# Hybrid mLSTM/attention encoder layer: which buffers hold the output projection's residual rows and its last norm scale, and what a held block waits for

## The chip, the cores and the metric

One core of one Trainium2 chip. The metric is the device time in microseconds (us) of one execution; runs of one kernel lie within about 0.3% of each other. Profile times are counted from the start of the profiled span.

## The reference

One encoder layer on two requests (2048 and 256 tokens, 2304 rows together, width 1024), all in float32:

```python
def encoder_layer(x, ...):
    h = rmsnorm(x, norm1_w)
    p = h @ w_in                                   # mq, mk, mv, mo, gates, aq, ak, av
    m_out = mlstm_mixer(mq, mk, mv, mo, gates, b_gates, mh_norm_w)   # 8 heads, both directions
    a_out = attention_mixer(aq, ak, av, q_norm_w, k_norm_w)          # 8 heads on 2 kv heads, all keys
    x = x + jnp.concatenate([m_out, a_out], axis=-1) @ w_out
    h = rmsnorm(x, norm2_w)
    u = centred_dwconv(h @ w_up, conv_w, conv_b)                     # width 3, 2 x 2816 channels
    a, g = jnp.split(u, 2, axis=-1)
    return x + (jax.nn.silu(g) * a) @ w_down       # a last rmsnorm follows
```

## The kernel before

The work is done in stages, each with its own pools of buffers, and every float32 matrix product is three products of rounded parts (high x high, low x high, high x low), so each operand is split by a ScalarE copy (the high part) and a VectorE subtraction (the low part).

- Stage a: norm statistics, queries, keys, values and gates.
- Stages b and m together: attention (`attention`, a generator over 36 blocks of one or two heads) and the mLSTM heads (`mlstm`). Both write their results to DRAM in `mix_d`.
- Stage c (`phase_c`): x + mix @ w_out. It goes over nine blocks of 256 tokens in the order `ORDER = (0, 1, 2, 3, 4, 5, 8, 6, 7)`; block 8 is the short request. It begins while attention still runs, and its matmuls fill TensorE between attention's.
- Stage d: the up-projection (`up_phase`, three token blocks of 768, each in 11 rounds `gi` of two pairs `UpPair`), with convolution and gate, and the down-projection.

**A block of stage c.** `loads` and `loads2` fetch eight tiles of mixed input (`mix`, L973 to L975: load, ScalarE copy, VectorE subtraction; blocks at even places of the order in the ring `nT`, at odd places in the ring `mx`, eight buffers each) and four tiles of x, each 128 x 512 (L985, ring `x`, `CX` = 6 buffers). `mm` makes four output slices z of 48 matmuls each (L997); two PSUM banks `po` take turns. `post` adds x to a slice on VectorE (L1004, the eviction of the bank), stores the sum to `x1_d` (L1005) and sums squares (L1007, L1011; ring `sq`, one buffer). `tail`, traced after the first slice of the block that follows, turns the sum into a scale (`rstd_bc`), multiplies the four x tiles by the norm weight and the scale (L1026) and stores them to `n2_d` (L1028). So an x buffer is free only when that store has landed.

**The last block's tail** (block 7) is `g.c_end`, called after the first matmuls of stage d (`first`, two `UpPair`s). Here `rstd_bc` runs with `act`: TensorE sums the squares (L128), ScalarE takes the root (L133), VectorE adds epsilon (L134), inverts the root and makes a Newton step (L138 to L141, tiles `rcol`, `rcol0`, `rcol1`). GpSimd stores the 256 scales to `rl_d` (L145), reads them back spread over all partitions into `rb` (L147, tag `sq`), and after ScalarE's weight (L1023) multiplies x by it (L1024) and stores it (L1028).

**Shared space.** A pool that opens takes the space of closed ones, and each new tile waits for the old tiles that lie under it. Stage c's pools lie on the right side of the buffer memory, from low to high: x, `mx`, `acc`, `sq`, the little `rcol` columns, `nT`, `raw` (weight loads), half of the weights. Stage d's first buffer of `u` (the evicted up-projection, L1168, six buffers) begins inside `acc` and ends just behind the `rcol` columns; the other five lie over `nT`. Its tiles of the gate (`y`, `ts`) lie over x and `mx`. Most operands of the first up-projections (L1087 to L1089) and the weight sums `tw` (L1122) lie over stage c's weights, so they wait for stage c's last matmul.

**The held block.** The first mixed input of the seventh block in order (block 8) is first written by a one-element cast on GpSimd (L972) from `g.hold`. `g.hold` is the tile `m4` (row maxima of the scores) of the attention block that called `prep2` last (L571), here the last of the 36; so block 8 isn't loaded before that tile is made.

**What orders the work.** Instructions are traced in program order with priorities and then put in each engine's queue by a planner that simulates the program's timeline (`schedule_with_timeline_sim`). A queue is in order: who waits holds up what is behind. Nearly all DMAs are issued by SyncE (SP).

Of the kernel before, what the change touches and what calls it, by code (L numbers as in the profile page):

```python
# [9 lines left out]
F32 = mybir.dt.float32  # L10
F32R = mybir.dt.float32r
AF = mybir.ActivationFunctionType
ALU = mybir.AluOpType
# [4 lines left out]
P = 128  # L18
# [9 lines left out]
EPS = 1e-6  # L28
# [8 lines left out]
BT = 256  # L37
NB = T // BT
NTB = 8
CX = 6  # L40
# [8 lines left out]
MXB = 8  # L49
# [13 lines left out]
ORDER = (0, 1, 2, 3, 4, 5, 8, 6, 7)  # L63
# [22 lines left out]
def f32(ap):  # L86
    return ap.bitcast(F32)
# [32 lines left out]
def rstd_bc(g, sp, pp, sqs, n, ptag, name, bufs=1, act=False):  # L120


    nc = g.nc
    k = n // P
    ps = pp.tile([P, 512], F32, tag=ptag, name="rs_" + name, bufs=bufs)
    for t in range(k):
        for i, sq in enumerate(sqs):
            nc.tensor.matmul(ps[:, 504 + 2 * t:506 + 2 * t], sq[:, t * P:(t + 1) * P], g.ones, start=i == 0,  # L128
                             stop=i == len(sqs) - 1)
    r = sp.tile([P, 4], F32, tag="rcol", name="rcol_" + name)[:, 0:k]  # L130
    if act:
        sr = sp.tile([P, 4], F32, tag="rcol0", name="rcol0_" + name, bufs=1)[:, 0:k]
        nc.scalar.activation(sr, ps[:, 504:504 + 2 * k].rearrange("p (t o) -> p t o", o=2)[:, :, 0], AF.Sqrt, bias=g.eps)  # L133
    nc.vector.tensor_scalar(r, ps[:, 504:504 + 2 * k].rearrange("p (t o) -> p t o", o=2)[:, :, 0], EPS, None, ALU.add)  # L134
    if act:
        v, r = r, sr
        u = sp.tile([P, 4], F32, tag="rcol1", name="rcol1_" + name, bufs=1)[:, 0:k]
        nc.vector.reciprocal(r, r)  # L138
        nc.vector.scalar_tensor_tensor(u, r, -0.5, r, ALU.mult, ALU.mult)
        nc.vector.tensor_tensor(u, u, v, ALU.mult)  # L140
        nc.vector.scalar_tensor_tensor(r, u, 1.5, r, ALU.add, ALU.mult)  # L141
    else:
        nc.gpsimd.tensor_tensor(r, r, g.mhalf[:, 0:k], ALU.pow)
    if act:
        nc.gpsimd.dma_start(g.rl_d.rearrange("t p -> p t"), r)  # L145
        rb = sp.tile([P, k, P], F32, tag="sq", name="rb_" + name, bufs=1)
        nc.gpsimd.dma_start(rb, g.rl_d[:].unsqueeze(0).to_broadcast([P, k, P]))  # L147
        return rb.rearrange("p t q -> p (t q)")
    for t in range(k):
        nc.tensor.matmul(ps[:, t * P:(t + 1) * P], r[:, t:t + 1].to_broadcast([P, P]), g.ident, start=True, stop=True)  # L150
    return ps[:, 0:n]
# [311 lines left out]
def attention(g, tc, s1, s2, pp):  # L463


    nc = g.nc
    sp = s1
    hbs = []
# [7 lines left out]
    def load_kv(grp, k0, k1, after=None):  # L476

        if (grp, k0) in kv:
            return
        n = k1 - k0  # L480
        sp = s2 if n == NT1 else s1
        kv[(grp, k0)] = parts = []
        for t0 in range(0, n, 4):
            m = min(4, n - t0)
            s = f"{n}_{t0}"
            kk = sp.tile([P, m * P], F32R, tag="kk" + s, name=f"kk{grp}_{s}", bufs=1)
            kl1 = sp.tile([65, m * P], F32R, tag="kl1" + s, name=f"kl1{grp}_{s}", bufs=1)
            vv = sp.tile([P, m, P], F32R, tag="vv" + s, name=f"vv{grp}_{s}", bufs=1)
            vl = sp.tile([P, m, HD], F32R, tag="vl" + s, name=f"vl{grp}_{s}", bufs=1)
            c = slice((k0 + t0) * P, (k0 + t0 + m) * P)  # L490
            if after is not None:
                for t in (kk[0:1, 0:1], kk[HD:HD + 1, 0:1], kl1[0:1, 0:1], vv[0:1, 0, 0:1], vl[0:1, 0, 0:1]):
                    nc.gpsimd.tensor_copy(t, after[0:1, 0:1])
            nc.gpsimd.memset(f32(vv[:, :, HD:P]), 1.0)
            for r in (0, HD):
                nc.gpsimd.dma_start(f32(kk[r:r + HD, :]), g.k_d[grp, 0:HD, c])
            nc.gpsimd.dma_start(f32(kl1[0:HD, :]), g.k_d[grp, HD:P, c])
            nc.gpsimd.memset(f32(kl1[64:65, :]), 1.0)
            for a, t in ((0, vv[:, :, 0:HD]), (1, vl)):
                nc.gpsimd.dma_start(f32(t), g.v_d[grp, :, k0 + t0:k0 + t0 + m, a])  # L500
            parts.append((kk, kl1, vv, vl))
# [14 lines left out]
    def load_q(n):  # L516

        if n in qzs or n >= len(hbs):
            return
        t = 0  # L520
        qz = qzs[n] = sp.tile([P, 4, P], F32R, tag="qz", name=f"bq{n}", bufs=QZB)
        for h, q0, q1 in hbs[n][1]:
            nc.sync.dma_start(f32(qz[:, t:t + q1 - q0]), g.q_d[h, q0:q1].rearrange("n p d -> p n d"))
            t += q1 - q0

    def prep(n):

        s = HB()
        grp, s.qs, k0, k1 = hbs[n]
        s.last = n == len(hbs) - 1  # L530
        load_q(n)
        load_kv(grp, k0, k1)
        s.kv = kv[(grp, k0)]
        s.nq, s.nk = 4, k1 - k0
        s.N = s.nq * P
        s.nm = "%d_%d" % s.qs[0][0:2]
        qz = qzs.pop(n)
        pq = pp.tile([P, 1024], F32R, tag="sc", name="pq" + s.nm)
        for t in range(s.nq):
            nc.tensor.transpose(pq[:, t * P:(t + 1) * P], qz[:, t, :], g.identr)  # L540
        load_q(n + 1)
        s.qq = sp.tile([P, 512], F32R, tag="qq", name="qq" + s.nm, bufs=2)
        nc.scalar.activation(s.qq[:, 0:s.N], f32(pq[:, 0:s.N]), AF.Copy)
        s.qm = sp.tile([65, 512], F32R, tag="qm", name="qm" + s.nm, bufs=2)
        nc.scalar.activation(s.qm[0:HD, 0:s.N], f32(pq[0:HD, 0:s.N]), AF.Copy)
        s.mx = sp.tile([P, 4, 2], F32, tag="mx", name="mx" + s.nm, bufs=2)
        s.nsp = -(-s.nk * P // 1024)
        s.todo = [(t, z) for z in range(s.nsp) for t in range(s.nq)] if s.nk * P > 512 else [(None, 0)]
        s.steps = len(s.todo)
        return s  # L550
# [17 lines left out]
    def prep2(s):  # L568

        nq = s.nq  # L570
        s.m4 = g.hold = sp.tile([P, 4], F32, tag="m4", name="m4" + s.nm, bufs=2)  # L571
        nc.vector.tensor_reduce(s.m4[:, 0:nq], s.mx[:, 0:nq, 0:s.nsp], AX.X, ALU.max)
        m4r = sp.tile([P, 4], F32R, tag="m4r", name="m4r" + s.nm, bufs=2)
        nc.vector.tensor_scalar(m4r[:, 0:nq], s.m4[:, 0:nq], -1.0, None, ALU.mult)
        pr = pp.tile([P, 1024], F32, tag="sc", name="pr" + s.nm)
        for t in range(nq):
            nc.tensor.matmul(pr[:, t * P:(t + 1) * P], m4r[:, t:t + 1].to_broadcast([P, P]), g.identr, start=True,
                             stop=True)
        nc.scalar.activation(s.qm[HD:HD + 1, 0:s.N], pr[HD:HD + 1, 0:s.N], AF.Copy)
# [28 lines left out]
    def fin1(s):  # L608

        s.o1 = sp.tile([P, 256], F32, tag="o1", name="o1" + s.nm, bufs=1)  # L610
        s.rs = sp.tile([P, 256], F32, tag="rs", name="rs" + s.nm, bufs=1)
        for z in range(2):
            for r, o in ((0, s.o1), (HD, s.rs)):
                nc.scalar.activation(o[HD * z:HD * z + HD], s.pv[r:r + HD, 256 * z:256 * z + 256], AF.Copy)  # L614

    def fin2(s):
# [6 lines left out]
        for h, q0, q1 in s.qs:  # L623
# [6 lines left out]
            if h == 5:  # L630
                g.mixed5.update(range(q0, q1))

    cur = prep(0)
    while cur.todo:
        maxstep(cur)
        yield 0.5
    prep2(cur)
    load_kv(0, 0, NT1, cur.m4)
    pend, fins = [], []
# [311 lines left out]
def phase_c(g, sn, sp, pp, wps):  # L951
# [3 lines left out]
    nc = g.nc  # L955
# [10 lines left out]
    def mix(b, c):  # L966
        if ORDER.index(b) % 2:
            m = sp.tile([P, 2, BT], F32R, tag="mx", name=f"cmx{b}_{c}", bufs=MXB)
        else:
            m = sn.tile([P, 2, BT], F32R, tag="nT", name=f"cmx{b}_{c}", bufs=NTB)  # L970
        if (b, c) == (ORDER[6], 0):
            nc.gpsimd.tensor_copy(m[0:1, 1, 0:1], g.hold[0:1, 0:1])  # L972
        nc.sync.dma_start(f32(m[:, 1]), g.mix_d[b, :, c])  # L973
        nc.scalar.activation(m[:, 0], f32(m[:, 1]), AF.Copy)
        nc.vector.tensor_tensor(m[:, 1], f32(m[:, 1]), f32(m[:, 0]), ALU.subtract)  # L975
        return m

    def loads(b):
        return [mix(b, c) for c in range(NCC - 1)]

    def loads2(b, mx):
        mx.append(mix(b, NCC - 1))
        x = [sp.tile([P, 2, BT], F32, tag="x", name=f"cx{b}_{z}", bufs=CX) for z in range(4)]
        for z in range(4):
            nc.sync.dma_start(x[z], g.xT[b, :, 2 * z:2 * z + 2])  # L985
        return x
# [50 lines left out]
    for i, b in enumerate(ORDER):  # L1037
        yield 2 * b
        mx = pre.pop(b) if b in pre else loads(b)
        x = loads2(b, mx)  # L1040
# [623 lines left out]
```

## Time and profile before

| | |
|---|---|
| median of 3 runs | 3342.4 us (3339.56 to 3344.06) |
| profiled execution | 3341.97 us, its span 3340.3 us |
| TensorE matmul busy | 3246.0 us (97%) |
| TensorE weight loads | 3021.6 us (90%) |
| VectorE, ScalarE, GpSimd | 2426.8 us (73%), 1996.0 us (60%), 532.2 us (16%) |
| mean granted TensorE clock | 0.988 |

The profile page gives busy time by engine, 40 slices of the span with busy shares in tenths, the chain of work that ended last, and groups of instructions by source line. Its trace can be asked for an engine's instructions in order of time, for who waited for whom, and for busy time in any stretch. In such rows `<-` behind a duration in brackets names what ended the idle time ahead of an instruction.

### The profile page before, as it was taken

The numbers are of one execution on the slowest core, as the hardware profiler recorded it, in microseconds if no ns is written. First come the engines' busy times: TensorE is split into PE (matmuls) and PEld (weight loads), VectorE is DVE, ScalarE is ACT, GpSimd is POOL, SyncE is SP. The second block draws the span as 40 slices with busy tenths as digits, with TensorE's granted clock in tenths as the row PEclk, the third lists the DMA queues.
The fourth block names the chain that finished last, engine by engine and source line by source line (L and its number), as shares of the span: only waits on it lengthen the run. The fifth ranks groups of instructions, "written<-read, shape, count | busy, mean of one in ns | idle before, by whom it ended". The sixth has DMA issues, their size and how long they took to land. (4 is left out here: it accounts for less than half of the span.)

```text
span 3340.3 us, 53168 instructions
## 1 busy us (share of the span) xinstructions
PE 3246.0 (97%) x19484; PEld 3021.6 (90%) x19484; DVE 2426.8 (73%) x3751; ACT 1996.0 (60%) x3746; POOL 532.2 (16%) x927
## 2 busy tenths in 40 slices
PE   8989999999999999999998799999999999999998
PEld 7888888888888888788878799999999999999998
DVE  7855676676657778866666699998888888666664
ACT  5646666666665666754563455666666677554543
POOL 4551042223224323100000100000000000020201
PEclk9999999999999999999999899999999999999999
DMA  9973333343355444422228466668676657967673
GB/s 351 316 213 100 110 100 116 101 119 117 91 159 171 126 147 136 134 86 96 96 65 282 162 237 217 220 235 278 211 255 237 209 194 253 316 226 269 217 243 122
DMA packets 359197, 612.44 MB, mean 183 GB/s; under 512 B 31077, under 2 KB 215319, under 8 KB 358935
## 3 DMA queue, kind: packets, MB, share of 16 engines
q1 hardware_dynamic: 329431, 563.14, 50.2%
q0 software_dynamic: 11936, 34.09, 3.8%
q10 hardware_dynamic: 17568, 11.80, 1.1%
q8 instruction: 154, 2.52, 0.3%
q14 instruction: 108, 0.88, 0.1%
HBM read 444.98 MB, written 163.93 MB: 182 GB/s over the span
## 5 line engine op out<-in xcount | busy, mean ns | idle before, releaser
L593 DVE TENSOR_TENSOR xx<-pe,xx 128x1024 fp32r<-128x1024 f32 x260 | 319.3, 1228 | 165.0 <-ACT xx L592 163.6
L591 ACT ACTIVATE pe<-ps 128x1024 f32<-128x1024 f32 x260 | 266.2, 1024 | 229.4 <-PE ps L588 215.3
L566 DVE TENSOR_REDUCE mx<-px 128x1 f32<-128x1024 f32 x256 | 310.7, 1219 | 100.9 <-PE px L564 99.8
L592 ACT ACTIVATE xx<-pe 128x1024 fp32r<-128x1024 f32 x260 | 275.0, 1058 | 5.1
L1381 POOL TENSOR_TENSOR sq<-sq,sq 128x384 f32<-128x384 f32 x38 | 49.2, 1295 | 1380.2 <-ACT sq L1377 1299.2
L997 PEld LDWEIGHTS po<-cmx,wo 128*128 128x128 f32 x1728 | 232.4, 192 | 26.3 <-issue 5.5
L997 PE MATMUL po<-cmx,wo 128*128 128x256 f32 x1728 | 240.9, 285 | 8.3 <-DVE cx L1004 7.4
L1168 ACT ACTIVATE u<-pa 128x386 f32<-128x386 f32 (+2 forms) x264 | 129.2, 490 | 197.1 <-PE pa L1164 172.5
L604 PE MATMUL pv<-xx,vv 128*128 128x512 f32 x520 | 212.5, 409 | 9.7 <-ACT rs L614 6.8
L587 PE MATMUL ps<-qq,kk 128*128 128x512 f32 x520 | 213.5, 411 | 7.8 <-ACT pe L591 3.7
L606 PE MATMUL pv<-xx,vv 128*128 128x512 f32 x520 | 210.8, 405 | 4.8 <-DVE xx L593 4.8
L588 PE MATMUL ps<-qm,kl 65*128 65x512 f32 x520 | 208.6, 401 | 0.0
L605 PE MATMUL pv<-xx,vl 128*64 128x512 f32 x520 | 207.4, 399 | 0.0
L722 PEld LDWEIGHTS mj<-mn,wm 128*128 128x128 f32 x1296 | 179.8, 194 | 18.4 <-ACT og L738 4.5
L722 PE MATMUL mj<-mn,wm 128*128 128x256 f32 x1296 | 191.1, 289 | 2.8 <-ACT og L738 2.8
L732 PE MATMUL mv<-wm,mn 128*128 128x256 f32 x1296 | 189.8, 286 | 1.4 <-ACT qb L728 1.4
L732 PEld LDWEIGHTS mv<-wm,mn 128*128 128x128 f32 x1296 | 176.1, 190 | 15.3 <-ACT qb L728 2.4
L243 PE MATMUL pj<-w_a,n1T 128*128 128x512 f32 (+1 forms) x864 | 166.5, 351 | 9.5 <-ACT w_a L105 7.6
L564 PE MATMUL px<-kk,qq 128*128 128x512 f32 x512 | 167.3, 408 | 2.5 <-ACT pe L591 2.4
L1164 PE MATMUL pa<-nt,wb 128*128 128x386 f32 (+2 forms) x792 | 148.3, 342 | 19.2 <-ACT u L1168 19.2
L243 PEld LDWEIGHTS pj<-w_a,n1T 128*128 128x128 f32 x864 | 140.3, 191 | 28.8 <-ACT w_a L105 7.6
L1164 PEld LDWEIGHTS pa<-nt,wb 128*128 128x128 f32 x792 | 142.1, 192 | 19.7 <-ACT u L1168 19.7
(341 smaller groups left out, 8069.6 us busy)
## 6 DMA issues: line engine op xcount, KB each, us to landing
mn<-n_d SPq DMA_DIRECT2D x216, 256.0 KB, 3.1
ru<-w_up SPq DMA_DIRECT2D x88, 512.0 KB, 4.9
rs<-wsu_d SPq DMA_DIRECT2D x88, 512.0 KB, 5.6
act_d<-ts SPq DMA_DIRECT2D x33, 768.0 KB, 6.2
nt<-act_d SPq DMA_DIRECT2D x60, 384.0 KB, 4.9
re_t<-wsd_d SPq DMA_DIRECT2D x45, 512.0 KB, 5.3
wsu_d<-tw SPq DMA_DIRECT2D x44, 512.0 KB, 3.5
act_d<-ya SPq DMA_DIRECT2D x99, 192.0 KB, 2.1
```

Of the source, the lines that this page charges most:

```text
L243: nc.tensor.matmul(pjs[t][:, c0:c1], nTs[tiles[t]][:, c, a, :], ws[c][:, b, c0:c1], start=(c == 0 and k == 0), stop=(c == NCC - 1 and k == 2))
L566: nc.vector.tensor_reduce(s.mx[:, t0, z0:z0 + 1], ps, AX.X, ALU.max)
L587: nc.tensor.matmul(o, kk[:, kc:kc + P], s.qq, start=True, stop=False)
L591: nc.scalar.activation(pe, ps, AF.Exp)
L592: nc.scalar.activation(x[:, 0], pe, AF.Copy)
L593: nc.vector.tensor_tensor(x[:, 1], pe, f32(x[:, 0]), ALU.subtract)
L604: nc.tensor.matmul(s.pv, vv[:, kt % 4, :], x1, start=kt == 0, stop=False)
L606: nc.tensor.matmul(s.pv, vv[:, kt % 4, :], x2, start=False, stop=kt == s.nk - 1)
L722: nc.tensor.matmul(pj[:, o].rearrange("p (n t) -> p n t", t=P), s.w[c][:, a, o * P:(o + 1) * P], nT[c][:, :, h, :], start=(c + o + k == 0) ...
L732: nc.tensor.matmul(pv[:, o], nT[c][:, o, a, :], s.w[c][:, h, 256:512], start=(c + o + k == 0), stop=(c == NCC - 1 and k == 2 and o == 1))
L997: nc.tensor.matmul(po[:, o], wo[c][z // 2][:, a, n], mx[c][:, h, :], start=c + o + k == 0, stop=c == NCC - 1 and o == 1 and k == 2)
L1164: s.nc.tensor.matmul(p, w[:, aa, c, :], ops[k][:, c, bb, 0:s.n], start=c == 0 and i == 0 and not add, stop=c == NCC // 2 - 1 and i == 2, s ...
```

## The change

- The last block's four x tiles are taken from the ring `mx` (the mixed inputs'), those of the block two places before (block 8) half from `x` and half from `raw`; all others stay in `x`.
- The spread scale `rb` of the last block is taken from `mx` instead of `sq`.
- In the same tail, ScalarE reads the sum out of PSUM: it adds epsilon (Identity into `r`) and takes the root of `r`; VectorE's addition is left to the other blocks.
- `g.hold` is no longer each block's `m4`; it is the output tile `o1` (one buffer) of the third-last attention block.

```diff
     if act:
         sr = sp.tile([P, 4], F32, tag="rcol0", name="rcol0_" + name, bufs=1)[:, 0:k]
-        nc.scalar.activation(sr, ps[:, 504:504 + 2 * k].rearrange("p (t o) -> p t o", o=2)[:, :, 0], AF.Sqrt, bias=g.eps)
-    nc.vector.tensor_scalar(r, ps[:, 504:504 + 2 * k].rearrange("p (t o) -> p t o", o=2)[:, :, 0], EPS, None, ALU.add)
+        nc.scalar.activation(r, ps[:, 504:504 + 2 * k].rearrange("p (t o) -> p t o", o=2)[:, :, 0], AF.Identity, bias=g.eps)
+        nc.scalar.activation(sr, r, AF.Sqrt)
+    else:
+        nc.vector.tensor_scalar(r, ps[:, 504:504 + 2 * k].rearrange("p (t o) -> p t o", o=2)[:, :, 0], EPS, None, ALU.add)
...
         nc.gpsimd.dma_start(g.rl_d.rearrange("t p -> p t"), r)
-        rb = sp.tile([P, k, P], F32, tag="sq", name="rb_" + name, bufs=1)
+        rb = f32(sp.tile([P, 2, BT], F32R, tag="mx", name="rb_" + name, bufs=MXB))[:, 0, 0:n].rearrange("p (t q) -> p t q", t=k)
...
         grp, s.qs, k0, k1 = hbs[n]
+        s.n = n
...
-        s.m4 = g.hold = sp.tile([P, 4], F32, tag="m4", name="m4" + s.nm, bufs=2)
+        s.m4 = sp.tile([P, 4], F32, tag="m4", name="m4" + s.nm, bufs=2)
...
         s.o1 = sp.tile([P, 256], F32, tag="o1", name="o1" + s.nm, bufs=1)
+        if s.n == len(hbs) - 3:
+            g.hold = s.o1
...
         mx.append(mix(b, NCC - 1))
-        x = [sp.tile([P, 2, BT], F32, tag="x", name=f"cx{b}_{z}", bufs=CX) for z in range(4)]
+        i = ORDER.index(b)
+        if i == NB - 1:
+            x = [f32(sp.tile([P, 2, BT], F32R, tag="mx", name=f"cx{b}_{z}", bufs=MXB)) for z in range(4)]
+        else:
+            x = [sp.tile([P, 2, BT], F32, tag="x", name=f"cx{b}_{z}", bufs=CX) for z in range(2 if i == NB - 3 else 4)]
+            x += [g.raw.tile([P, 512], F32, tag="raw", name=f"cx{b}_{z}", bufs=2).rearrange("p (o t) -> p o t", o=2)
+                  for z in range(len(x), 4)]
```

## The prediction

> **What bounds the kernel now.** I read the page first (busy shares, the slices), then the chain that ended last, then stretches, TensorE's order of time around the one dip, and there the queues of the other engines.
>
> ```profile
> span 3340.3 us, 53168 instructions
> PE 3246.0 (97%) x19484; PEld 3021.6 (90%) x19484; DVE 2426.8 (73%) x3751; ACT 1996.0 (60%) x3746; POOL 532.2 (16%) x927
> PE   8989999999999999999998799999999999999998
> PEclk9999999999999999999999899999999999999999
> ```
>
> TensorE is busy 97% of the span, and the order of its work is fixed, so time comes off only where it idles or runs at a lower clock. The dip in slices 22 and 23 (about 1750 to 1920 us) is the passage from the output projection (stage c) to the up-projection (stage d). All that the diff touches stands there.
>
> ```profile
> core 0: us, PE busy (x), PEclk, DMA share, GB/s
> 1690.00:1718.50 28.50, 22.90 (x92) 1.00 0.38 117
> 1752.20:1821.30 69.10, 61.70 (x494) 0.95 0.78 267
> 1790.60:1796.00 5.40, 0.08 (x2) 0.95 0.98 337
> 1796.00:1798.00 2.00, 2.00 (x9) 0.50 0.87 308
> 1841.80:1861.00 19.20, 0.03 (x1) 0.50 0.06 7
> 1861.00:1864.00 3.00, 3.00 (x9) 0.50 0.66 225
> 1880.00:2820.00 940.00, 940.00 (x5352) 1.00 0.66 229
> ```
>
> Columns: stretch, its length, TensorE's busy time and matmuls, granted clock, DMA share, rate. Three holes: 5.6 us at the end of attention, one of 5.3, one of 19.2; behind the last two the clock is 0.50. The up-projection has no slack at all. TensorE's own rows name the releasers (in brackets: idle before, and what ended it):
>
> ```profile
> 1777.06 5.67 PE L997 MATMUL po<-cmx,wo 128*128 128x256 f32 x33 [2.08 <-DVE cx L1004]
> 1795.98 7.25 PE L997 MATMUL po<-cmx,wo 128*128 128x256 f32 x48 [5.32 <-DVE cx L1004]
> 1807.44 13.79 PE L997 MATMUL po<-cmx,wo 128*128 128x256 f32 x114
> 1837.56 4.23 PE L1164 MATMUL pc<-nt,wb 128*128 128x386 f32 x12 [3.95 <-DVE rcol_c L134]
> 1860.97 7.32 PE L1164 MATMUL pa<-nt,wb 128*128 128x386 f32 x24 [19.18 <-ACT u L1168]
> ```
>
> Undisturbed, a matmul of stage c takes 13.79/114 = 0.121 us. Stage c's matmuls end at 1807.44 + 13.79 = 1821.2; I call that point E.
>
> **The change part by part.**
>
> **1. x of the last three blocks (8, 6, 7 in stage c's order).** Before, x has six buffers and each block takes four, so block 6 gets two of its x only when block 8's normed x has been stored.
>
> ```profile
> SPq L985 <- DMA n_d<-cx: 2.7, 4, 1.9
> 1790.73 0.48 DMA cx<-xT
> 1795.14 0.70 DVE cx L1004
> 1790.25 0.96 DVE L1089 TENSOR_TENSOR nt<-nt 128x772 fp32r<-128x772 f32 x1
> ```
>
> SP waits four times for that store; the load goes out at 1790.73, and the eviction that needs it (L1004) runs at 1795.14. That is the 5.32 us. After it, blocks 8 and 6 hold 2 + 4 = 6 x buffers and block 8 two raw ones, which stage c's weights left long ago: block 6's four loads wait for block 5 alone. The last block's x goes where block 6's mixed input was, free in its last output slice (z=3). Its first eviction is wanted two slices (96 x 0.121 = 11.6 us) after its first matmul, so there is time for a load like the one above (4.4 us). Removed: 5.32, and the slow restart, 7.25 - 48 x 0.121 = 1.4. Lower end: the eviction stands in VectorE's queue behind the row of 1790.25, which ends at 1791.21; with 0.7 for itself TensorE would still idle 1.3. Ends: -6.7 and 0 (another late input); I take **-6.0**, nearest the row that frees it all. Number of DMAs and their bytes are unchanged, and two loads leave the crowded stretch (DMA share 0.98).
>
> Such a rest of 1.3 us would, by the Trainium skill (TensorE: Matmul & The Clock Gate, "Part 1: The HAM clock gate"), cost no clock, since the gate closes after an idle window of about 3.4 us. The trace disagrees: behind 2.08 us of idleness 33 matmuls took 5.67 us, 1.7 more than 33 x 0.121. By the page this part would be -5.4 at worst, by the row -3.7.
>
> **2. The 2.08 us before it** come from VectorE's queue, not from a buffer of the change:
>
> ```profile
> 1775.06 0.75 DVE L975 TENSOR_TENSOR cmx<-cmx 128x256 fp32r<-128x256 f32 x2
> 1776.32 0.68 DVE L1004 TENSOR_TENSOR cx<-po,cx 128x512 f32<-128x512 f32 x1
> ```
>
> Block 6's first eviction stands behind the last block's mixed input, which waits for block 8's matmuls. Those come earlier (part 3), so up to 2.08 + 1.7 = 3.8 can go; it can as well grow by as much as the planner puts ahead of the eviction. Ends -3.8 and +2; **-1.5**.
>
> **3. The kept block.** Block 8's first mixed input waits for a one-element cast on GpSimd that reads the tile `hold`: before, the last attention block's maxima (L572), afterwards the third-last one's output (written last by L620).
>
> ```profile
> 1699.08 0.42 DVE L620 TENSOR_TENSOR o<-o,rs 128x256 f32<-128x256 f32 x1
> 1713.87 0.15 DVE L572 TENSOR_REDUCE m<-mx 128x4 f32<-128x8 f32 x1
> 1714.15 0.18 POOL L972 CAST cmx<-m 1x1 fp32r<-1x1 f32 x1 [13.05 <-DMA cmx<-mix_d]
> 1707.03 0.49 PE L604 MATMUL pv<-xx,vv 128*128 128x512 f32 x1 [0.36 <-ACT xx L592]
> 1708.50 0.50 PE L587 MATMUL ps<-qq,kk 128*128 128x512 f32 x1 [0.76 <-DVE mx L566]
> 1711.92 0.51 PE L604 MATMUL pv<-xx,vv 128*128 128x512 f32 x1 [0.36 <-ACT xx L592]
> 1714.01 0.50 PE L606 MATMUL pv<-xx,vv 128*128 128x512 f32 x1 [1.35 <-DVE xx L593]
> 1730.04 0.38 ACT L614 ACTIVATE o<-pv 64x256 f32<-64x256 f32 x1
> ```
>
> The cast can go at 1699.5 instead of 1714.0, some 14.5 us earlier, and block 8's matmuls fill TensorE from about 1704 on. The four idle gaps after that sum to 0.36 + 0.76 + 0.36 + 1.35 = 2.8; those before stay. TensorE works without a hole from there to the end of attention, so filler used earlier is not missed later. The output tile has one buffer, so the next block's copy (L614, 1730.04) now waits for the cast: 30 us of room. Ends -2.8 and 0; **-2.5**.
>
> **4. The spread scale and the first u.** The scale rb shared the buffer of the squares, and the first u of stage d lies over that buffer (pool order and sizes in the code).
>
> ```profile
> 1835.23 0.26 ACT L133 ACTIVATE rcol_c<-rs_c,eps 128x2 f32<-128x2 f32 x1
> 1838.74 0.17 DVE rcol_c L141
> 1841.87 8.15 DMA rl_d<-rcol_c
> 1850.66 0.58 POOL L147 DMA_DIRECT2D rb_c<-rl_d  x1 [8.02 <-DMA rl_d<-rcol_c]
> 1854.90 5.49 POOL L1024 TENSOR_TENSOR cx<-cx,rb_c 128x256 f32<-128x256 f32 x8 [3.67 <-DMA rb_c<-rl_d]
> 1860.42 0.88 ACT L1168 ACTIVATE u<-pa 128x386 f32<-128x386 f32 x2 [23.40 <-POOL cx L1024]
> ```
>
> ScalarE's copy into u starts 0.03 us after GpSimd's eighth multiply with rb (1854.90 + 5.49 = 1860.39). With rb in a mixed-input buffer that wait goes. What is late next: the same u also covers the little columns behind the squares, rcol0 among them, which the store to rl_d reads. So u waits for that store to land: 1841.87 + 8.15 = 1850.0, then, as now, 0.4 for ScalarE and 0.55 to TensorE's restart: 1851.0 instead of 1860.97, **-10.0**. Ends: -23.1 (this hole and the 3.95 before it both gone) and 0 (something as late in its place). The restart at half clock stays, since about 9 us of idleness are left. The later y and ts tiles over the mixed-input buffers are written after a whole round; I cost them at nothing.
>
> The store writes single elements; the fit in the Trainium skill (DMA: Bandwidth & Descriptors), 2.0 us plus bytes over 436e3 per us, gives an estimate of 2 us, and with it u would be ready near 1844, part 4 at -16. This store's own row, 8.15, decides.
>
> **5. The sum read by ScalarE.** One Identity like the 0.26 us Sqrt is added ahead of it, one 0.15 us VectorE operation (L134) goes, and the bank that holds up TensorE at 1837.56 is free after that Identity, near 1835.5. But TensorE then only reaches the wait for u sooner. The chain to rl_d is set by VectorE's queue (L141 at 1838.74); upper end -1.9, the way from Sqrt's end (1835.49) to 1837.4, lower +0.3: **0**.
>
> **6. Crowding.** From 1752.2 to 1821.3 DMA is 0.78 x 69.1 = 54 us busy; parts 1 to 3 leave some 59 us for it. Operands for the first up-projections, all loaded at E, start behind more traffic: 0 to +3, **+1**.
>
> Sum: -6.0 - 1.5 - 2.5 - 10.0 + 0 + 1 = -19.0. The profiled execution took 3341.97 us, its span and 1.7 around it; 3341.97 - 19.0 = 3323.0. The median before, 3342.4, is 0.4 above it, so I say **3323**.
>
> **The rivals.**
>
> A. *u waits for nothing on GpSimd's side*, because the planner hands that place to a later u. For: only the first u of the phase lies there. Against: buffers were taken in this order before. The hole shrinks to what VectorE's operand splits leave: some 13 us more gain, **3310**.
>
> B. *The x stall is replaced*: SP issues in order, and the last block's x waits there for block 6's matmuls with other loads behind it, or evictions stand behind splits in VectorE's queue as in part 2. Parts 1 and 2 are lost: **3331**.
>
> C. *The change doesn't free u*: it stays blocked as long by another tile over it. Against: the 0.03 us between GpSimd's last multiply and u. Parts 1 to 3 remain: **3333**; with B too, 3340, no change.
>
> D. *Slower*: the planner orders the whole program anew, and the first of the three token blocks of the up-projection has little room on VectorE:
>
> ```profile
> 1880.00:2200.00 320.00, 320.00 (x1810) 319.85 (x1809) 299.51 (x382) 196.25 (x308) 0.00 (x0) 1.00 0.63 220
> ```
>
> Columns: TensorE, its weight loads, VectorE, ScalarE, GpSimd. VectorE is 299.5 of 320 us busy while TensorE never waits. If evictions come to stand behind splits there, each of the eleven rounds gains a hole. It takes (19.0 + 6.7)/11 = 2.3 us a round to be slower; at 3 us a round, **3356**. Against: nothing there is edited, and the order before had no hole in 940 us.
>
> **How the numbers follow.** Forecast 0.54 (its own range 3316 to 3331), A 0.13, B 0.14, C 0.08, B with C 0.04, D 0.07. The bound of what can be told from no change is 0.2%, 6.7 us. Faster: forecast, A, B and most of C, 0.86; same: the rest of C, and B with C, 0.07; slower: D, 0.07. The range 3309 to 3337 leaves out D, B with C, and the lower end of A: 0.16.
>
> **What would show it.** Right: no idle time before the last block's matmuls and loads of block 6's x well before 1790; the cast near 1700; the first u copy released by the store to rl_d, some 29 us after stage c's last matmul instead of 39; multiplies with rb running beside u. Wrong: ScalarE's first u still released by GpSimd; another releaser of 4 to 5 us before the last block; holes between 1880 and 2820.

## The result, and the profile after

The changed kernel takes 3325.2 us (median of 5 runs, 3321.4 to 3327.5) against 3342.4 of the kernel before (5 runs): a ratio of 0.9943, 95% interval 0.9926 to 0.9960. The forecast was 3323, within 3309 to 3337. One execution of a later kernel (the scale alone) took 7148.9 us, more than twice any other; it stands in no ratio.

From the page of the changed kernel: the span, the busy shares, and TensorE's busy share and granted clock in 40 slices.

```profile
span 3323.5 us, 53157 instructions
PE 3240.1 (97%) x19484; PEld 3015.5 (91%) x19484; DVE 2427.3 (73%) x3750; ACT 1993.5 (60%) x3747; POOL 533.2 (16%) x927
PE   8989999999999999999999899999999999999998
PEclk9999999999999999999999899999999999999999
```

The two slices of the dip (8 and 7 tenths) are now one slice of 8. TensorE's rows in order of time through that passage, and one stretch of the up-projection (TensorE, its weight loads, VectorE, ScalarE, GpSimd):

```profile
1777.43 4.78 PE L1008 MATMUL po<-cmx,wo 128*128 128x256 f32 x38 [1.29 <-DVE cx L1015]
1782.41 13.33 PE L1008 MATMUL po<-cmx,wo 128*128 128x256 f32 x110
1799.72 13.56 PE L1008 MATMUL po<-cmx,wo 128*128 128x256 f32 x112
1823.31 4.45 PE L1175 MATMUL pc<-nt,wb 128*128 128x386 f32 x24
1843.34 6.59 PE L1175 MATMUL pa<-nt,wb 128*128 128x386 f32 x24 [15.59 <-ACT u L1179]
```
```profile
1880.00:2820.00 940.00, 940.00 (x5354) 939.86 (x5353) 827.55 (x1013) 613.16 (x1071) 0.00 (x0) 1.00 0.67 231
```

The 5.32 us hole ahead of the last block is gone: 110 matmuls run through its start, and between 1735 and 1787 SP issues no load of x. The 3.95 us ahead of the pc group is gone as well. From E (now 1799.72 + 13.56 = 1813.28) to the restart it is 30.06 us instead of 39.74. The up-projection still has no hole, which disposes of rival D. The other engines at the two places where the change acts:

```profile
1704.49 0.80 POOL L145 TENSOR_TENSOR rcol_c<-rcol_c,mhalf 128x2 f32<-128x2 f32 x1 [43.67 <-DVE rcol_c L136]
1705.27 1.08 POOL L631 DMA_DIRECT2D mix_d<-o  x2
1706.36 0.70 POOL L977 CAST cmx<-o 1x1 fp32r<-1x1 f32 x1
...
1834.84 0.77 POOL L147 DMA_DIRECT2D rl_d<-rcol_c  x1 [37.72 <-issue]
1848.07 8.39 POOL L1035 TENSOR_TENSOR cx<-cx,rb_c 128x256 f32<-128x256 f32 x8 [4.26 <-issue]
```
```profile
1842.80 0.88 ACT L1179 ACTIVATE u<-pa 128x386 f32<-128x386 f32 x2 [12.42 <-DMA rl_d<-rcol_c]
```

The first u starts 5.3 us before the multiplies with rb begin, and is released by the store to rl_d, as forecast.

One thing does not fit. The engines' orders of instructions first differ near 1428 us (two loads of x on SP), and yet the changed kernel is 5.5 us late already at 1409. As a milestone near attention's end I take one of ScalarE's copies out of attention's last matmuls (the 67th; M below): 1691.04 before, 1696.36 after, so 5.3 us lost ahead of the kept block's cast and all that follows. The profile therefore has to be read in segments: M to E, E to TensorE's restart R (the start of the first group pa<-nt,wb), R to the end of the span. All profiles of this study (us):

| kernel | M | M to E | E to R | R to end | span |
|---|---|---|---|---|---|
| before | 1691.0 | 130.2 | 39.7 | 1479.3 | 3340.3 |
| before, again | 1697.2 | 131.0 | 40.3 | 1478.8 | 3347.4 |
| changed | 1696.4 | 116.9 | 30.1 | 1480.2 | 3323.5 |
| changed, again | 1700.1 | 119.1 | 30.7 | 1480.4 | 3330.3 |
| x alone | 1694.2 | 121.1 | 40.4 | 1477.7 | 3333.3 |
| scale alone | 1699.1 | 131.4 | 29.7 | 1484.7 | 3344.9 |
| sum alone | 1691.0 | 131.5 | 40.0 | 1478.4 | 3340.8 |
| kept block alone | 1692.3 | 125.8 | 40.4 | 1475.1 | 3333.6 |
| one column moved | 1694.4 | 117.1 | 19.3 | 1489.8 | 3320.6 |
| three columns moved | 1689.3 | 116.1 | 17.5 | 1489.3 | 3312.2 |
| clear of the first y | 1690.7 | 116.2 | 17.4 | 1478.3 | 3302.5 |
| tie to the fifth-last | 1701.6 | 116.8 | 32.3 | 1476.6 | 3327.2 |
| tie to the fourth-last | 1696.7 | 123.0 | 28.5 | 1477.8 | 3326.0 |

In the last two rows M itself is moved by the edit: 532 and 561 of stage c's matmuls come behind it, 576 in the kernels before and changed, so their M and M to E can't be compared with the other rows.

### The profile page after: what moved, and what is told of

Its sections match the earlier page's. It is cut to its first block, busy times and chain, and to the rows that moved or that the text cites. A ratio compares the mean times of both kernels' runs of the same rounds, so it can differ in the third digit from the quotient of the medians.

```text
span 3323.5 us, 53157 instructions
## 1 busy us (share of the span) xinstructions
PE 3240.1 (97%) x19484; PEld 3015.5 (91%) x19484; DVE 2427.3 (73%) x3750; ACT 1993.5 (60%) x3747; POOL 533.2 (16%) x927
## 5 line engine op out<-in xcount | busy, mean ns | idle before, releaser
L607 PE MATMUL pv<-xx,vv 128*128 128x512 f32 x520 | 212.5, 409 | 11.3 <-ACT rs L619 7.1
L245 PEld LDWEIGHTS pj<-w_a,n1T 128*128 128x128 f32 x864 | 141.5, 192 | 30.7 <-ACT w_a L105 7.4
```

The source lines that it names most:

```text
L245: nc.tensor.matmul(pjs[t][:, c0:c1], nTs[tiles[t]][:, c, a, :], ws[c][:, b, c0:c1], start=(c == 0 and k == 0), stop=(c == NCC - 1 and k == 2))
L607: nc.tensor.matmul(s.pv, vv[:, kt % 4, :], x1, start=kt == 0, stop=False)
```

## The experiments

My theory (W) was that each edit is worth the wait that it removes; the rival (O), that the planner's new order made the gain and the edits only pay together. All ratios are to the kernel before.

**The kernels before and after, once more.** No edit.

> The kernel before, unchanged, profiled once more. In the two profiles shown, the changed kernel reaches the 67th of ScalarE's copies out of attention's last matmuls (ACT o<-pv; 1691.04 before, 1696.36 after) 5.3 us later, though no engine's order of instructions differs up to there. Theory V (executions of one program differ by some us up to there, whatever the kernel): this profile shows that copy at another time than 1691.04, by 1 to 8 us, while the way from that copy to stage c's last matmul (130.2), from there to TensorE's restart (39.7) and from the restart to the end of the span (1479.3) repeat within 1.5 us each. Theory L (the lag belongs to the changed program, its placing in memory): 1691.0 within 0.5. Time 3340 to 3349 by either.

> The changed kernel once more, unchanged, in the same call as the two kernels beside it. Theory V (executions of one program differ by some us on the way to attention's end, whatever the kernel): the 67th of ScalarE's copies out of attention's last matmuls comes at another time than 1696.4, anywhere from 1689 to 1700, while the way from there to stage c's last matmul (116.9), from that to TensorE's restart (30.1) and on to the end (1480.2) repeat within 1.5 us. Theory L (the lag is the changed program's own): 1696.4 within 0.5. Time 0.9926 to 0.996 of before.

Ratios: 1.0001 (0.9992 to 1.0010) and 0.9939 (0.9927 to 0.9952). M, in the two profiles of each program, before first:

```profile
1691.04 0.36 ACT L614 ACTIVATE o<-pv 64x256 f32<-64x256 f32 x1
```
```profile
1697.24 0.36 ACT L614 ACTIVATE o<-pv 64x256 f32<-64x256 f32 x1
```
```profile
1696.36 0.36 ACT L619 ACTIVATE o<-pv 64x256 f32<-64x256 f32 x1
```
```profile
1700.13 0.36 ACT L619 ACTIVATE o<-pv 64x256 f32<-64x256 f32 x1
```

M differs by 6.2 us between two executions of the unchanged kernel and by 3.8 between two of the changed one; over the eleven profiles in which the edits leave M alone it lies between 1689.3 and 1700.1. Its mean is 1694.1 over the six of the kernel before and the single edits, and 1694.2 over the five of the changed kernel and those built on it. So the 5.3 us are not the change's (theory V). The later segments of the unchanged kernel repeat within 0.9 us, those of the changed one within 0.6 except M to E, 2.2 longer the second time, more than the 1.5 that I allowed. That is the short wait ahead of block 6's first eviction:

```profile
1781.88 6.29 PE L1008 MATMUL po<-cmx,wo 128*128 128x256 f32 x38 [1.83 <-DVE cx L1015]
```

1.83 us idle instead of 1.29, and 38 matmuls in 6.29 us instead of 4.78: 2.1 together. What causes M's variation stays open.

**Each edit alone, on the kernel before.** The x buffers (the kernel with only that hunk of the diff):

```
...
+        if i == NB - 1:
+            x = [f32(sp.tile([P, 2, BT], F32R, tag="mx", ...)) for z in range(4)]
...
+            x += [g.raw.tile([P, 512], F32, tag="raw", ...)... for z in range(len(x), 4)]
```

> The kernel before with one edit of the four: x of the last three blocks in the two raw buffers and in buffers of mixed inputs. Theory W (each edit is worth the wait that it removes): the 5.32 us hole ahead of the last block's matmuls and the slow restart behind it go, 6 to 8 us less from block 6's first matmul to the end of stage c (before 1777.06 to 1821.23, 44.2 us; now 36 to 38); the first u copy of stage d is still released by GpSimd's multiplies with rb, some 39 us after stage c's last matmul. Time 3334 to 3337. Theory O (what gained is that the planner put the program into another order, and the edits only pay together): the hole is replaced by another of 3 to 5 us, time 3340 to 3343.

Ratio 0.9980 (0.9971 to 0.9989): 3337.5 us, with 3345.1 for the kernel before measured beside it. TensorE's rows:

```profile
1779.40 4.19 PE L1003 MATMUL po<-cmx,wo 128*128 128x256 f32 x33 [1.06 <-DVE cx L1010]
1783.79 14.52 PE L1003 MATMUL po<-cmx,wo 128*128 128x256 f32 x120
1802.30 12.97 PE L1003 MATMUL po<-cmx,wo 128*128 128x256 f32 x107
1855.65 7.23 PE L1170 MATMUL pa<-nt,wb 128*128 128x386 f32 x24 [19.77 <-ACT u L1174]
```

From block 6's first matmul to E 1815.27 - 1779.40 = 35.9 us, M to E 9.1 less than before, E to R 40.4 instead of 39.7. That is W, with a step 0.1 us shorter and a time 0.5 us longer than it named.

The spread scale:

```
-        rb = sp.tile([P, k, P], F32, tag="sq", name="rb_" + name, bufs=1)
+        rb = f32(sp.tile([P, 2, BT], F32R, tag="mx", ...))[:, 0, 0:n]...
```

> The kernel before with one edit: the spread scale rb in a buffer of mixed inputs instead of that of the squares. Theory W: the first u copy is released by the landing of the store to rl_d and not by GpSimd's multiplies; from stage c's last matmul to TensorE's restart some 30 us instead of 39.7; the 5.32 us hole stays. Time 3332 to 3333. Theory O: the first u is released by GpSimd as before, time 3340 to 3343.

Ratio 0.9982 (0.9972 to 0.9991), 3340.1 us: 6 us less by the ratio, where W's price was 10. Four of its executions take 3332.9 to 3333.6 us, close to W's 3332 to 3333, and six 3339.2 to 3346.6; what parts them stays open. The segments say why the profiled one, the longest of these (3346.6 us), shows no gain at all: M came 8.1 us later than in the first profile before, and R to the end took 5.4 us more. The step itself gained what was forecast:

```profile
1803.96 8.52 PE L997 MATMUL po<-cmx,wo 128*128 128x256 f32 x48 [5.79 <-DVE cx L1004]
...
1816.70 13.79 PE L997 MATMUL po<-cmx,wo 128*128 128x256 f32 x114
...
1860.16 6.41 PE L1164 MATMUL pa<-nt,wb 128*128 128x386 f32 x24 [9.52 <-ACT u L1168]
...
1890.72 6.05 PE L1164 MATMUL pa<-nt,wb 128*128 128x386 f32 x24 [2.09 <-ACT u L1168]
```
```profile
1859.61 0.88 ACT L1168 ACTIVATE u<-pa 128x386 f32<-128x386 f32 x2 [13.27 <-DMA rl_d<-rcol_c]
...
1883.57 1.03 ACT L1285 ACTIVATE yg<-u,cw 128x768 f32<-128x768 f32 x1 [4.83 <-DMA n_d<-cx]
```

E (1830.49) to R 29.7 us instead of 39.7, and u is released by the store to rl_d; the x hole is still there. The last row of each engine tells why R to the end is longer. The last block's x still lies in the ring x here, and ScalarE's first write of stage d's tile yg waits 4.83 us for the store of its normed rows (n_d<-cx). The copies of u behind it come late, and TensorE idles 2.09 us ahead of the second round and restarts slowly. The down-projection's first matmul follows R by 968.1 us, in the two profiles before by 964.3 and 963.3; the rest of the 5.4 us lies behind it.

The sum:

```
-        nc.scalar.activation(sr, <sum>, AF.Sqrt, bias=g.eps)
-    nc.vector.tensor_scalar(r, <sum>, EPS, None, ALU.add)
+        nc.scalar.activation(r, <sum>, AF.Identity, bias=g.eps)
+        nc.scalar.activation(sr, r, AF.Sqrt)
...
```

> The kernel before with one edit: the sum of squares read by ScalarE (Identity, then Sqrt) instead of by ScalarE and VectorE. Theory W: the 3.95 us idle ahead of the pc matmuls goes or shrinks, since VectorE no longer has to read that bank, but the first u is still released by GpSimd's multiplies, which end at most 1 us earlier: time 3341 to 3343. Rival: the chain behind the sum starts earlier too, by as much as the 3.95 us: time 3338 to 3339.

Ratio 1.0006 (0.9998 to 1.0015).

```profile
1835.57 2.38 PE L1166 MATMUL pc<-nt,wb 128*128 128x386 f32 x12 [0.76 <-ACT rcol_c L133]
1862.44 6.13 PE L1166 MATMUL pa<-nt,wb 128*128 128x386 f32 x24 [24.49 <-ACT u L1170]
```

The hole ahead of pc shrinks from 3.95 to 0.76 and the next one grows from 19.18 to 24.49, and E to R is 40.0: a wait off the path, moved and not saved.

The kept block:

```
-        s.m4 = g.hold = sp.tile([P, 4], F32, tag="m4", ...)
+        s.m4 = sp.tile([P, 4], F32, tag="m4", ...)
...
+        if s.n == len(hbs) - 3:
+            g.hold = s.o1
```

> The kernel before with one edit: the kept block is tied to the third-last attention block's output. Theory W: the cast goes near 1700 to 1707 instead of 1714, some 35 to 55 of stage c's matmuls move ahead of the end of attention, and 2.5 to 4 us of idle time there go: time 3338 to 3340. Rival: the filler used earlier is missed later, or block 6's x, which still waits for block 8's store, is no earlier, so that the 5.32 us hole grows by what was gained: time 3341 to 3343.

Ratio 0.9990 (0.9981 to 0.9999), 3339.2 us. Stretch from M to the end of block 8's matmuls (column order as above), in the kernel before and in this one:

```profile
1691.04:1774.47 83.43, 78.10 (x468) 64.54 (x469) 52.97 (x75) 45.06 (x63) 3.08 (x6) 1.00 0.34 110
```
```profile
1692.34:1771.76 79.42, 76.71 (x468) 64.85 (x469) 51.35 (x75) 43.37 (x63) 3.60 (x6) 1.00 0.32 100
```

The same 468 matmuls in 79.4 us instead of 83.4. Idle time falls from 5.33 to 2.71, and busy time by another 1.4 (the profile models the ends of matmuls, so the sum is surer than the split). The rival's later loss is not shown: the x hole, which this kernel keeps, is 5.93 instead of 5.32 and the 48 matmuls behind it take 8.19 us instead of 7.25, but in the other kernels that keep it, the one before again among them, these are 5.13 to 6.14 and 8.13 to 8.65.

Up to R the single edits add up, each against the first profile before: M to E -9.1 (x) and -4.4 (kept block), together -13.5, against -13.3 and -11.1 in the two profiles of the changed kernel; E to R -10.1 (scale), against -9.7 and -9.1. So theory O falls for these waits. Behind R it holds in part: alone, the scale edit loses some 4 us again to yg's wait, which the changed kernel doesn't have. The whole times are too coarse to test the sum: the four ratios add up to -14 us, with about 3 us of uncertainty each, against -19 and -20 for the changed kernel.

**What u waits for next.** The changed kernel with rcol0, which the store to rl_d reads, in a mixed-input buffer, and then with all three columns there:

```
-        sr = sp.tile([P, 4], F32, tag="rcol0", ...)[:, 0:k]
+        sr = f32(sp.tile([P, 2, BT], F32R, tag="mx", ...))[:, 0, 0:k]
```

> The changed kernel with one more edit: the column that the store to rl_d reads (rcol0) lies in a buffer of mixed inputs too, so that the first u of stage d no longer lies over anything that GpSimd's stores read; it still lies over two columns that VectorE writes and reads. Theory W (u waits for the store to rl_d and for nothing else as late): u is released by VectorE's last operation on the columns, at 1831.9 on the changed kernel's clock, and TensorE restarts near 1832.7 instead of 1843.3: from stage c's last matmul to the restart 19 to 20 us instead of 30.1; time 10 to 11 us below the changed kernel's, 0.990 to 0.992 of before. Rival S (something else is as late: the operands of those matmuls, or the loads behind that store): the restart moves by less than 4 us, or the matmuls behind it run with holes that give the gain back; time 0.993 to 0.995 of before.

> The changed kernel with all three columns (rcol, rcol0, rcol1) in buffers of mixed inputs, so that the first u waits neither for GpSimd's store nor for VectorE's chain of columns. Theory W: ScalarE's own queue sets u, at about 1830.4 on the changed kernel's clock; TensorE restarts 17.5 to 19 us after stage c's last matmul (30.1 in the changed kernel); time 11 to 13 us below the changed kernel's, 0.989 to 0.991 of before. Rival S: as for the kernel with one column moved; then this one is no faster than that.

Ratios 0.9929 (0.9917 to 0.9942) and 0.9929 (0.9916 to 0.9943): their intervals overlap the changed kernel's. TensorE's rows of the first and then the second kernel, and the second one's ScalarE and GpSimd:

```profile
1830.79 6.68 PE L1175 MATMUL pa<-nt,wb 128*128 128x386 f32 x24 [4.73 <-ACT u L1179]
...
1867.88 6.89 PE L1175 MATMUL pa<-nt,wb 128*128 128x386 f32 x24 [8.73 <-ACT u L1179]
```
```profile
1822.87 4.51 PE L1178 MATMUL pa<-nt,wb 128*128 128x386 f32 x24 [3.02 <-ACT u L1182]
...
1859.87 7.24 PE L1178 MATMUL pa<-nt,wb 128*128 128x386 f32 x24 [11.31 <-ACT u L1182]
```
```profile
1854.78 1.03 ACT L1299 ACTIVATE ya<-u,cw 128x768 f32<-128x768 f32 x1 [15.01 <-issue]
```
```profile
1849.40 2.98 POOL L1042 DMA_DIRECT2D n_d<-cx  x4
```

The restart came as W said (E to R 19.3 and 17.5 us), so the store to rl_d did hold u. But W's times (0.989 to 0.992) were missed, as rival S had it: a second hole of 8.7 or 11.3 us opens and gives most of the gain back (R to end +9 us). In the second kernel ScalarE stands 15 us in front of its first write of ya, until 2.4 us after the last store of the normed x was issued; in the first one the profile names that store as the releaser. The layout has the reason: the first ya lies over the buffer in which the x edit put the last slice of the last block's x. In the changed kernel ScalarE comes to ya only at 1863.6 and waits there too, but no more than 2.5 us, since those stores were issued by 1859.4, and TensorE loses nothing by it. The first kernel's row and then the changed one's:

```profile
1862.80 1.03 ACT L1296 ACTIVATE ya<-u,cw 128x768 f32<-128x768 f32 x1 [11.10 <-DMA n_d<-cx]
```
```profile
1866.06 1.03 ACT L1296 ACTIVATE ya<-u,cw 128x768 f32<-128x768 f32 x1 [2.50 <-issue]
```

So the slice and the scale were moved under tiles that stage d writes only in its second round, and the columns under the first yg:

```
...
+            g.cols = sp.tile([P, 2, BT], F32, tag="x", name="cols", bufs=CX)
+            nc.gpsimd.tensor_copy(g.cols[0:1, 0, 0:1], g.mhalf[0:1, 0:1])
+            x = [f32(sp.tile([P, 2, BT], F32R, tag="mx", ...)) for z in range(3)]
+            x.append(sp.tile([P, 2, BT], F32, tag="x", name=f"cx{b}_3", bufs=CX))
...
+        rb = sp.tile([P, 2, BT], F32, tag="x", name="rb_" + name, bufs=CX)[:, 0, 0:n]...
```

> The kernels with one and with three moved columns restarted 19 and 17.5 us after stage c's last matmul, but TensorE then idled 8.7 and 11.3 us more, both times until ScalarE's first copy into the tile ya of stage d. That tile (160928 to 167072 in the layout) lies over the buffer that the changed kernel gives to the last slice of the last block's x (165792 to 167840), and ya began 2.4 us after the last store of that x was issued. This kernel moves the three columns, the spread scale and that one slice of x so that none lies under what stage d writes in its first round: the slice at 153504 and the scale at 151456 (under y tiles of the second round), the columns under the first yg, with a one-element copy on GpSimd ahead of them. Theory Y (ya waits for that slice's store): ya begins within 6 us of yg, the second hole goes or falls under 4 us, TensorE restarts 17 to 20 us after stage c's last matmul and the next pa<-nt,wb group of the second round starts 42 to 47 us after it (58.0 in the changed kernel, 54.5 with three columns moved); time 0.988 to 0.991 of before. Rival Q (ya waits for GpSimd's queue or the crowd of transfers, not for that tile): the second hole stays at 8 to 11 us and the time at 0.992 to 0.994.

Ratio 0.9882 (0.9869 to 0.9896), 3306.7 us: faster than both kernels. TensorE's and ScalarE's rows:

```profile
1824.22 6.03 PE L1178 MATMUL pa<-nt,wb 128*128 128x386 f32 x24 [2.88 <-ACT u L1182]
...
1851.28 4.41 PE L1178 MATMUL pa<-nt,wb 128*128 128x386 f32 x24
```
```profile
1839.33 1.03 ACT L1299 ACTIVATE yg<-u,cw 128x768 f32<-128x768 f32 x1 [0.36 <-ACT carry L1298]
...
1841.40 1.01 ACT L1299 ACTIVATE ya<-u,cw 128x768 f32<-128x768 f32 x1
```

ya follows yg by 2.1 us, the second hole is gone, and the second round's group starts 1851.28 - 1806.83 = 44.5 us after E. Theory Y holds. Three things moved together, so it is the row of 11.10 us above, and not this kernel alone, that names the store of x. GpSimd's stores go out as late as ever (1857.5); TensorE no longer waits for them, VectorE's first ts waits 1.45 us.

**The tie further back.** The changed kernel with `len(hbs) - 5` and with `len(hbs) - 4`:

> The changed kernel with the kept block tied to the fifth-last attention block's output instead of the third-last one's. Theory W (the kept block gains by filling TensorE's short waits with stage c's matmuls): the cast goes earlier, to between 1620 and 1690, the waits of 0.4 to 0.6 us that the changed kernel still shows ahead of 1705 (0.42, 0.55, 0.56, 0.48) go too, 1 to 3 us from there to stage c's last matmul; time 0.9934 to 0.994 of before. Rival: GpSimd's queue holds the cast up behind the stores of the block before, or the filler used earlier is missed later: no gain or a loss of up to 3 us.

> The changed kernel with the kept block tied to the fourth-last attention block's output. With the fifth-last one's, no short wait was left from 1616 to the end of attention, but then TensorE idled 9.1 us for the last block's last input, since the matmuls that could have covered it had been used up: only 300 of stage c's matmuls were left behind attention (423 in the changed kernel). Theory F (the filler is finite): with the fourth-last one, more than 340 are left, the hole behind attention stays under 4 us, and the time is 0.993 to 0.9945 of before, no more than 3 us from the changed kernel's. Rival: each attention block by which the tie moves back gains its own 2 us, so that the time falls to 0.9925 or below.

Ratios 0.9948 (0.9936 to 0.9961) and 0.9950 (0.9936 to 0.9963): no better than the changed kernel. The first one's theory W fell, and its rival came, a wait behind attention. The row behind the end of attention, fifth-last and then fourth-last:

```profile
1780.03 20.32 PE L1008 MATMUL po<-cmx,wo 128*128 128x256 f32 x156 [9.08 <-ACT cmx L979]
```
```profile
1780.15 21.53 PE L1008 MATMUL po<-cmx,wo 128*128 128x256 f32 x156 [10.61 <-ACT cmx L979]
```

The theory of a finite filler holds in its direction (earlier use is missed at the end, for the input that only attention's last output completes), but its numbers for the fourth-last tie fell: 300 matmuls are left there too, and the hole is 10.6 us, not under 4, and the time is just above its 0.9945. The planner's order steps from one arrangement to the other between the third-last and the fourth-last block.

## Why the prediction was right, point by point

- **Total.** Forecast -19.0. The two profiles of each program from M on: before 1649.3 and 1650.2, changed 1627.1 and 1630.2, a mean of -21.1. The ratio gives -19.1 (-24.7 to -13.4). That its middle falls on the forecast is luck: parts 1 to 3 came out larger than forecast in the first profile, part 6 did not come, and the two changed profiles give -22.1 and -19.1 from M on against the first one before. That the first changed span is only 16.8 shorter is M's variation.
- **Part 1, x: -6.0; measured -6.7**, the end that I had set for the case that everything goes: the 5.32 us hole and its slow restart are gone, in the changed kernel and with the x edit alone. In the second profile before, the two together were 8.0.
- **Part 2, the stall before: -1.5; measured -2.3 in the one profile and -0.2 in the other.** The wait fell from 2.08 to 1.29 and 1.83. Most of the difference is the clock: with 1.29 the slow matmuls behind it (1.7) go too. The reason that I gave, block 8's earlier matmuls, is not needed: the x edit alone brings 1.06, the kept block alone 1.65.
- **Part 3, kept block: -2.5; measured -4.0 (kept block alone).** This is the term that was mis-sized most. I left out the wait ahead of block 8's first matmuls, 0.93 us in this row of the kernel before,

```profile
1718.47 1.91 PE L997 MATMUL po<-cmx,wo 128*128 128x256 f32 x12 [0.93 <-ACT cmx L974]
```

  and I counted idle time alone, while the same matmuls also show 1.4 us less busy time. The cast went at 1706.4 instead of 1699.5. Of the 6.9 us between, 5.3 are M's lateness and 1.6 GpSimd's queue: a power and two stores stand ahead of the cast.
- **Part 4, scale: -10.0; measured -9.7 and -10.1 (changed kernel, scale alone)**, with the wait that I named as the next one, the store to rl_d. In the changed kernel it took 7.9 us from its issue, 1834.84, and in the second profile 8.5. The estimate of 2 us from the fit in the Trainium skill (DMA: Bandwidth & Descriptors, "Anatomy of one DMA") is contradicted for this store. What failed is the zero for the tiles y and ts: the first yg and ya are written within the first round, and ScalarE waited 2.5 us for the place of ya. That TensorE lost nothing by it is luck, as the two kernels with moved columns show.
- **Part 5, sum: 0; measured 0** (E to R 40.0 alone; 39.7 and 40.3 before).
- **Part 6, crowding: +1; R to the end +0.8 and +1.1 against the first profile before**, no more than the other kernels scatter. The mechanism that I gave did not show: the first pc group, which reads the operands loaded at E, starts 10.0 us behind E before (1831.27) and after (1823.31).
- **Rival A** would have needed more than I gave it. I priced u free of GpSimd at 3310 and 13 us of further gain. Forced, it gave two kernels whose whole-time gain on the changed one the intervals do not separate, because I looked at the first tile over GpSimd's data and not at the next, ya. With both cleared, E to the end fell from 1510.2 to 1495.7, by 14.6 us. B, C and D did not happen.

## What to carry over

When a tile is moved out of one later tile's way, list everything that the next stage writes over its new place, in order of time: here the x buffers that removed a 5 us wait put the last x under the next stage's second tile, where it held up ScalarE by 2.5 us and, once the wait ahead of it was taken away, TensorE by 9 to 11; without that edit the same x held up the next stage's first tile. Where a kernel's executions differ by 6 us ahead of the change, compare segments between fixed instructions and not spans. Work kept back to fill short waits is worth moving forward only while enough of it is left for the last late input.

## What the runs showed of the hardware that I had not expected

How much a short wait of TensorE costs is not its length alone. Ahead of block 6's first eviction, length separates the cases: behind the five waits of 1.77 to 2.08 us in these profiles the next 33 or 38 matmuls took about 1.7 us more than at 0.121 us each, behind the six of 1.06 to 1.65 us at most 0.2 more. Ahead of the first group pa<-nt,wb it does not. Granted clock (third number from the end) just behind a wait of 1.83 us (changed kernel again), 1.65 us (kept block alone), 3.02 us (three columns) and 2.88 us (clear of the first y):

```profile
1781.88:1784.00 2.12, 2.12 (x12) 2.12 (x13) 2.12 (x4) 1.72 (x4) 0.49 (x1) 0.62 1.00 361
```
```profile
1773.90:1776.00 2.10, 2.08 (x17) 2.08 (x18) 2.10 (x4) 2.08 (x4) 0.45 (x1) 1.00 1.06 382
```
```profile
1822.80:1825.00 2.20, 2.13 (x12) 2.14 (x13) 2.13 (x7) 2.20 (x6) 0.00 (x0) 1.00 0.88 350
```
```profile
1824.20:1827.00 2.80, 2.78 (x9) 2.78 (x10) 2.66 (x8) 2.15 (x5) 0.00 (x0) 0.56 0.71 281
```

After 3.02 us of waiting 24 matmuls took 4.51 us, full speed (4.45 undisturbed); after 2.88 us they took 6.03. The Trainium skill (TensorE: Matmul & The Clock Gate, "Part 1: The HAM clock gate") has the activity window run freely, so that the point of change depends on where in the window a matmul lands; the pair would fit that, but no run here shows the window. By the same section of the Trainium skill the slow clock comes after at least one idle window of about 3.4 us; the clock of 0.62 behind 1.83 us contradicts that.
